# Pool products between the value products, and the eighth square as a second term of the first and last norm's sum

## The chip, the cores and the metric

One core of a Trainium2 chip. The metric is the device time of one execution in microseconds (us); less is better. PE is TensorE's matmul, PEld its weight load, DVE VectorE, ACT ScalarE, SP the queue that issues most DMAs. Times inside the profile count from the start of its span.

## The reference, cut to what matters

Two transformer blocks over one sequence of 256 tokens and 1024 features, in fp32. The change touches the first mixer of the first block and two of its seven RMS norms:

```python
def pool_attn_mixer(h, w_in, pool_w, pool_scale, q_gain, k_gain, w_out):
    u, q, k, v = jnp.split(h @ w_in, [512, 1024, 1536], axis=-1)
    p = multiscale_pool_minus_identity(u)       # 4 groups of 128 channels: mean of the last 2, 4, 8, 16 tokens, minus u
    p = jnp.einsum('bsgc,gcd->bsgd', p.reshape(B, S, 4, 128), pool_w)   # one 128x128 matrix per group
    p = p.reshape(B, S, 512) * pool_scale
    a = moba_attention(q, k, v, q_gain, k_gain) # 8 heads of 64; with 256 tokens plain causal attention
    return jnp.concatenate([p, a], axis=-1) @ w_out

def rms_norm(x, g):
    return x * lax.rsqrt(jnp.mean(x * x, axis=-1, keepdims=True) + EPS) * g
```

Every norm needs, for each token, the sum of the squares of its 1024 features. The first norm stands ahead of this mixer, the last one at the very end of the program.

## The kernel before

**Layout.** Activations lie transposed: features on the 128 partitions, eight blocks of them, tokens along the row (`T` = 256). `X` holds the residual. An fp32 product is made of three fp32r products: a weight tile and an activation are each split into `hi` (an ACT copy) and `lo` (a DVE subtract of `hi` from the source). `mm3` issues hi·hi (L280), hi·lo (L281) and lo·hi (L282) into one accumulator. `split_act` splits an activation: L342 or, with a scale, L336 on ACT, then L322 or L331 on DVE.

**Weights.** They come as a stream of 128x128 tiles in the order in which the program asks for them (`W`, which appends to `order`). Eight tiles are a half chunk p; `w_split(p)` splits it with one ACT cast (L246) and one DVE subtract (L322, 128x1024) into one of `NB` = 5 pairs of buffers hi0/lo0 to hi4/lo4, in rotation. When the first tile of half chunk p is asked for, `W` issues the split of p+4, so that split uses the buffers of half chunk p-1. The splits of half chunks 16 to 20 fall into the stretch of the change and are called split 16 to split 20 here. In the kernel before, half chunk 15 holds the weights of value products k = 6 and 7, and half chunk 16 the four pool weights and the first four of `pa_out`.

**Buffers.** `al` and `alp` take one of 46 SBUF slots, `bk` one of eight PSUM banks, each from the front of a first-in first-out list; `fr` and `bf` put them back at the end. A new holder of a buffer waits until every instruction that uses the former holder is done, those written later in the program included.

**Order.** A scheduler places the instructions when the program is built: for each engine it keeps dependencies and, among those it takes to be ready, prefers the one written first. What stands in an engine's queue then runs in that order. `step` advances the attention by one iteration, and `behind` (with `PINNED`, which is DVE) ties every DVE instruction of that iteration behind the DVE instruction that was written last before it:

```python
        for ins in reversed(done):
            if ins.engine in engines and ins.engine not in last:
                last[ins.engine] = ins.name
```

**The stretch of the change** is in `mixer0`. After the products for k, q and u come the value products: eight steps k, each with two token halves and three products of 512 columns (L285), in banks `vb`. Among them, at k = 0, 2, 4, 6, `windows` makes the pool inputs of one group on DVE (running sums of 2, 4, 8, 16 tokens, times 1/count, minus u). `step` is called after k = 3 (head 0's logits, `att_a(0)`) and after k = 7 (`att_b(0)`: reciprocal and scaling on DVE, transposes on PE, copy on ACT; `att_a(1)`). Then the four pool inputs are split into `px`, `step` is called once more (`att_c(0)`, `att_b(1)`, `att_a(2)`), then for each pair of groups six pool products go into one bank, and four results are split with the pool scale into `pp`. `pp[k]` is the input of `pa_out` for k = 0 to 3, the attention's output that for k = 4 to 7. `acc_begin` takes four banks for `pa_out`: output blocks m = 0,1 in the first, 2,3 in the second, 4,5 in the third, 6,7 in the fourth.

**The norm.** `norm_add(m)` squares block m on ACT (L373) and adds the square to `sacc` on DVE (L322); `norm_sum` multiplies `sacc` with a matrix of 1/1024 (two fp32 matmuls of one column, L285), which sums over the partitions. `self.gain` is None for the first and the last norm alone. In the last one, `turn(m)` scales each block (L1823) and transposes it on PE (L1825) right after `norm_add(m)`.

Of the kernel before, what the change touches and what calls it, by code (L numbers as in the profile page):

```python
# [12 lines left out]
OP = mybir.AluOpType  # L13
# [3 lines left out]
T = 256  # L17
D = 1024
KD = 8
# [117 lines left out]
class Prog:  # L137
# [137 lines left out]

    def mm3(self, out, key, x, start, stop):

        wh, wl = self.W(key)
        mm = self.nc.tensor.matmul
        mm(out, wh, x[0], start=start, stop=False, skip_group_check=True)  # L280
        mm(out, wh, x[1], start=False, stop=False, skip_group_check=True)  # L281
        mm(out, wl, x[0], start=False, stop=stop, skip_group_check=True)  # L282

    def mm(self, out, l, r, start=True, stop=True):
        self.nc.tensor.matmul(out, l, r, start=start, stop=stop, skip_group_check=True)  # L285
# [78 lines left out]
    def norm_add(self, m):  # L364
        nc = self.nc
        acc = self.sacc[:, :T]
        if self.gain is not None:
            self.split_act(self.X[:, m, :], *self.xgo(m), scale=self.gain(m))
        if self.nsq == 0:
            nc.scalar.activation(acc, self.X[:, m, :], AF.Square)  # L370
        else:
            sq = self.sqb[:, (self.nsq % 2) * T:(self.nsq % 2) * T + T]
            nc.scalar.activation(sq, self.X[:, m, :], AF.Square)  # L373
            self.tt(acc, acc, sq, OP.add)
        self.nsq += 1

    def norm_sum(self, sqrt=False):


        b = self.bk()  # L380
        for h in range(2):
            self.mm(b[:, h:h + 1], self.sacc[:, h * 128:h * 128 + 128], self.ones[:, 0:1], h == 0, True)
        self.uid += 1
        v = self.cst([128, 2], f"nv{self.uid}")
        self.ts(v, b[:, 0:2], EPS, OP.add)
        self.bf(b)
        if sqrt:
            y, t = self.cst([128, 2], "nry"), self.cst([128, 2], "nrt")
            self.nc.scalar.activation(y, v, AF.Sqrt)
            self.nc.vector.reciprocal(y, y)  # L390
            self.stt(t, y, -0.5, y, OP.mult, OP.mult)
            self.tt(t, t, v, OP.mult)
            self.stt(y, t, 1.5, y, OP.add, OP.mult)
            self.rtok = y
        else:
            self.rtok = self.rsqrt_small(v, 2, f"nr{self.uid}")
        self.fr(self.sacc, self.sqb)
# [127 lines left out]
    def mixer0(self):  # L525
# [39 lines left out]
        for b in range(4):  # L565
            sq = self.al()
# [34 lines left out]
        for b in range(2):  # L601
            p = self.bk()
            for i in range(2):
                for h in range(2):
                    for g in range(2):
                        o = h * 16 + (2 * b + i) * 2 + g
# [82 lines left out]
                yield  # L689
        self.lanes[0].append(attention())  # L690

        pin = []

        def windows():
            for g in range(4):
                s = self.al(shape=(128, 2, T))
                u = us[g // 2][:, g % 2, :]
                cur = u
                for e in range(g + 1):
                    d = 1 << e  # L700
                    nxt = s[:, e % 2, :]
                    self.tt(nxt[:, d:], cur[:, d:], cur[:, :T - d], OP.add)
                    nc.vector.tensor_copy(nxt[:, :d], cur[:, :d])
                    cur = nxt
                o = s[:, (g + 1) % 2, :]
                self.tt(o, cur, ivs[g // 2][:, (g % 2) * T:(g % 2) * T + T], OP.mult)
                self.tt(o, o, u, OP.subtract)
                pin.append((s, o))
                yield
        win = windows()  # L710
        vb = [self.bk(), self.bk()]
        vt = [self.al() for t in range(2)]
        for k in range(KD):
            wh, wl = self.W(("pa_v", k, 0), n=4)
            for t in range(2):
                xh, xl = (x[:, t * 128:t * 128 + 128] for x in self.hl(hs[k]))
                self.mm(vb[t], xh, wh, k == 0, False)
                self.mm(vb[t], xl, wh, False, False)
                self.mm(vb[t], xh, wl, False, k == KD - 1)
            if k in STEPS0:  # L720
                self.step()
            if k % 2 == 0:
                next(win)
        for t in range(2):
            nc.scalar.activation(vt[t], vb[t], AF.Copy, scale=rtok[:, t:t + 1])
            self.bf(vb[t])
        self.fr(*hs)
        px = []
        for g in range(4):
            x = self.alp()  # L730
            self.split_act(pin[g][1], *self.hl(x))
            self.fr(pin[g][0])
            px.append(x)
        self.fr(*us, *ivs)
        self.step()
        pp = []
        for b in range(2):
            p = self.bk()
            for i in range(2):
                self.mm3(p[:, i * T:i * T + T], ("pool_w", 0, 2 * b + i), self.hl(px[2 * b + i]), i == 0, True)  # L740
            for i in range(2):
                x = self.alp()
                self.split_act(p[:, i * T:i * T + T], *self.hl(x), scale=self.pv("pscale", 2 * b + i))
                pp.append(x)
            self.bf(p)
        self.fr(*px)
        xs = pp + ath
        self.acc_begin()
# [1235 lines left out]
```

## Time and profile before

| | |
|---|---|
| median of 3 runs | 1043.2 us (1041.69 to 1044.56) |
| the profiled execution | 1046.05 us, of which its span 1044.3 us |
| PE busy | 97% of the span |
| DVE, ACT busy | 83%, 58% |
| granted TensorE clock, mean | 0.995 |
| PE's waits between 20 and 100 us | 1.5 us in two pieces |

Busy PE time counts a matmul from its start to its modelled end, and neighbours overlap: products of 256 columns that follow one another closely start every 0.12 us though each is shown as 0.28 us long. So it is the distance of starts that tells whether PE runs dense, and the idle time in brackets that tells where it waited.

### The profile page before, as it was taken

Reading aid. Unit: us, or ns where it says so; the run is one execution under the profiler, and the core shown is the slowest. Engines: PE = TensorE matmul, PEld = TensorE weight load, DVE = VectorE, ACT = ScalarE, POOL = GpSimd, SP = SyncE. Lnnn points to the kernel's source line nnn. Section 1 sums busy time; section 2 is a strip of 40 time slices with the busy share of each in tenths; the row PEclk is TensorE's granted clock in tenths of the full one; section 3 lists DMA queues with packets and bytes.
Section 4 is the critical chain, followed back from the end, with each engine's and each line's share of the span. In section 5 each row is a group of like instructions: output and inputs, shape, how many; then the busy total and the mean of one; then the engine's idle time right before and its main releaser. Section 6 shows DMA issues by size and latency. Waiting matters only on the chain. (4 is left out here: it accounts for less than half of the span.)

```text
span 1044.3 us, 21508 instructions
## 1 busy us (share of the span) xinstructions
PE 1015.2 (97%) x8834; PEld 980.9 (94%) x8834; DVE 865.7 (83%) x1662; ACT 605.3 (58%) x953; POOL 96.8 (9%) x86
## 2 busy tenths in 40 slices
PE   9999999999999999999999999889999999999996
PEld 8879999999999999999999998778999999999996
DVE  6887999997799998999999978997667979775554
ACT  6566665565669975665654687233345457444444
POOL 0000000000000000000295000334200200000000
PEclk9999999999999999999999999999999999999999
DMA  8953367886682263777654644234454464955531
GB/s 310 353 186 119 125 207 272 305 314 223 211 281 95 71 235 120 241 255 269 225 202 153 241 149 149 72 116 146 145 198 162 154 206 142 386 172 192 191 133 41
DMA packets 32499, 202.75 MB, mean 194 GB/s; under 512 B 3601, under 2 KB 5137, under 8 KB 9233
## 3 DMA queue, kind: packets, MB, share of 16 engines
q1 hardware_dynamic: 31392, 199.80, 54.2%
q10 hardware_dynamic: 1008, 1.58, 0.4%
q8 instruction: 69, 1.13, 0.4%
q14 instruction: 30, 0.24, 0.1%
HBM read 200.32 MB, written 1.05 MB: 193 GB/s over the span
## 5 line engine op out<-in xcount | busy, mean ns | idle before, releaser
L281 PE MATMUL b<-s,hi 128*128 128x256 f32 x2192 | 616.9, 282 | 1.8 <-DVE s L331 0.9
L280 PE MATMUL b<-s,hi 128*128 128x256 f32 x2128 | 600.6, 283 | 4.8 <-ACT s L342 3.0
L282 PE MATMUL b<-s,lo 128*128 128x256 f32 x2128 | 598.2, 282 | 4.1 <-DVE lo L322 4.0
L322 DVE TENSOR_TENSOR lo<-raw,hi 128x1024 fp32r<-128x1024 f32 (+1 forms) x309 | 389.8, 1266 | 112.1 <-ACT hi L246 111.2
L246 ACT CAST hi<-raw 128x1024 fp32r<-128x1024 f32 (+1 forms) x309 | 319.8, 1041 | 261.4 <-PE b L281 185.4
L281 PEld LDWEIGHTS b<-s,hi 128*128 128x128 f32 x2192 | 413.4, 189 | 6.0 <-issue 3.0
L280 PEld LDWEIGHTS b<-s,hi 128*128 128x128 f32 x2128 | 400.6, 189 | 12.2 <-issue 4.0
L282 PEld LDWEIGHTS b<-s,lo 128*128 128x128 f32 x2128 | 400.9, 189 | 6.8 <-DVE lo L322 5.8
L322 DVE TENSOR_TENSOR s<-s,s 128x256 f32<-128x256 f32 (+3 forms) x173 | 89.2, 524 | 8.0 <-ACT s L373 3.7
L331 DVE SCALAR_TENSOR_TENSOR s<-b,pvt,s 128x255 f32<-128x255 f32 (+1 forms) x153 | 72.6, 478 | 3.8 <-ACT s L880 2.8
L461 DVE SCALAR_TENSOR_TENSOR ada<-ada,s 128x512 f32<-128x512 f32 x96 | 63.9, 685 | 3.6 <-DMA ada<-in_ada_dram 3.6
L285 PE MATMUL b<-xgh,hi 128*128 128x256 f32 (+1 forms) x212 | 60.5, 285 | 0.0
L285 PE MATMUL b<-s,hi 128*128 128x256 f32 x212 | 59.6, 281 | 0.0
L285 PE MATMUL b<-xgh,lo 128*128 128x256 f32 (+1 forms) x212 | 59.6, 281 | 0.0
L342 ACT CAST s<-s 128x256 fp32r<-128x256 f32 (+1 forms) x77 | 33.0, 440 | 37.0 <-DVE s L322 26.6
L880 ACT ACTIVATE s<-b,pvt 128x256 f32<-128x256 f32 x76 | 42.0, 556 | 8.5 <-PE b L282 8.2
L285 PE MATMUL b<-s,s 128*128 128x256 f32 (+5 forms) x212 | 39.2, 380 | 7.9 <-DVE s L322 7.4
L1174 POOL MEMSET tab<- 128x8 f32 x1 | 0.1, 113 | 494.2 <-DVE ada L461 494.2
L285 PEld LDWEIGHTS b<-s,hi 128*128 128x128 f32 x212 | 40.1, 189 | 0.0
L285 PEld LDWEIGHTS b<-xgh,lo 128*128 128x128 f32 x212 | 40.0, 189 | 0.0
L285 PEld LDWEIGHTS b<-xgh,hi 128*128 128x128 f32 x212 | 39.9, 188 | 0.0
L322 DVE TENSOR_TENSOR s<-s 128x256 f32<-128x256 f32 (+3 forms) x70 | 35.4, 508 | 4.7 <-ACT s L1790 4.3
(367 smaller groups left out, 1042.3 us busy)
## 6 DMA issues: line engine op xcount, KB each, us to landing
raw<-in_wst_dram SPq DMA_DIRECT2D x157, 1024.0 KB, 5.0
ada<-in_ada_dram SPq DMA_DIRECT2D x24, 1024.0 KB, 7.4
raw<-in_wst_dram SPq DMA_DIRECT2D x4, 512.0 KB, 6.4
s<-in_catt_dram SPq DMA_DIRECT2D x8, 192.0 KB, 7.2
s<-in_rgw_dram SPq DMA_DIRECT2D x5, 256.0 KB, 3.7
raw<-in_wst_dram SPq DMA_DIRECT2D x4, 256.0 KB, 5.5
xp<-in_xt_dram ACTq DMA_DIRECT2D x3, 256.0 KB, 6.1
s<-in_cinv_dram SPq DMA_DIRECT2D x2, 256.0 KB, 5.5
```

The source lines that it names most:

```text
L246: self.nc.scalar.copy(h, s)
L280: mm(out, wh, x[0], start=start, stop=False, skip_group_check=True)
L281: mm(out, wh, x[1], start=False, stop=False, skip_group_check=True)
L282: mm(out, wl, x[0], start=False, stop=stop, skip_group_check=True)
L285: self.nc.tensor.matmul(out, l, r, start=start, stop=stop, skip_group_check=True)
L322: self.nc.vector.tensor_tensor(out, a, b, op=op)
L331: self.nc.vector.scalar_tensor_tensor(out, a, s, b, op0=op0, op1=op1)
L342: nc.scalar.copy(hi, src)
L461: self.nc.vector.scalar_tensor_tensor(x, x, 0.5, self.cs[h], op0=OP.mult, op1=OP.mult, accum_out=self.macc[:, h, i:i + 1])
L880: nc.scalar.activation(c[:, i, :], z, AF.Identity, scale=self.pv(f"fcw{l}2", m), bias=self.pv(f"fcb{l}", m))
L1174: g.memset(S[:, :, 0:1], 0.0)
```

## The change

The four pool weights are taken ahead of value products k = 7, and the six pool products of groups 0 and 1 with their splits stand there too; those of groups 2 and 3 follow the value products. The windows move from k = 0, 2, 4, 6 to k = 0, 1, 2, 4, and each window now splits its own input. Half chunk 15 so holds the weights of k = 6 and the pool weights, half chunk 16 those of k = 7. In the first and the last norm the eighth square is not added to `sacc`; `norm_sum` takes it as a second term with two more matmuls.

```diff
@@ -275,7 +275,10 @@
     def mm3(self, out, key, x, start, stop):
-        wh, wl = self.W(key)
+        self.mm3w(out, self.W(key), x, start, stop)
+
+    def mm3w(self, out, w, x, start, stop):
+        wh, wl = w
         mm = self.nc.tensor.matmul
@@ -371,15 +374,18 @@
             nc.scalar.activation(sq, self.X[:, m, :], AF.Square)
-            self.tt(acc, acc, sq, OP.add)
+            if self.nsq < 7 or self.gain is not None:
+                self.tt(acc, acc, sq, OP.add)
...
         b = self.bk()
-        for h in range(2):
-            self.mm(b[:, h:h + 1], self.sacc[:, h * 128:h * 128 + 128], self.ones[:, 0:1], h == 0, True)
+        terms = [self.sacc] if self.gain is not None else [self.sacc, self.sqb[:, T:]]
+        for n, s in enumerate(terms):
+            for h in range(2):
+                self.mm(b[:, h:h + 1], s[:, h * 128:h * 128 + 128], self.ones[:, 0:1], n + h == 0, n == len(terms) - 1)
@@ -705,12 +711,29 @@
                 self.tt(o, o, u, OP.subtract)
-                pin.append((s, o))
+                x = self.alp()
+                self.split_act(o, *self.hl(x))
+                self.fr(s)
+                px.append(x)
                 yield
         win = windows()
         vb = [self.bk(), self.bk()]
         vt = [self.al() for t in range(2)]
+        pp = []
+
+        def pool(b):
+            p = self.bk()
+            for i in range(2):
+                self.mm3w(p[:, i * T:i * T + T], pw[2 * b + i], self.hl(px[2 * b + i]), i == 0, True)
+            for i in range(2):
+                x = self.alp()
+                self.split_act(p[:, i * T:i * T + T], *self.hl(x), scale=self.pv("pscale", 2 * b + i))
+                pp.append(x)
+            self.bf(p)
         for k in range(KD):
+            if k == KD - 1:
+                pw = [self.W(("pool_w", 0, m)) for m in range(4)]
+                pool(0)
             wh, wl = self.W(("pa_v", k, 0), n=4)
@@ -719,30 +742,15 @@
             if k in STEPS0:
                 self.step()
-            if k % 2 == 0:
+            if k in (0, 1, 2, 4):
                 next(win)
+        pool(1)
         for t in range(2):
             nc.scalar.activation(vt[t], vb[t], AF.Copy, scale=rtok[:, t:t + 1])
             self.bf(vb[t])
         self.fr(*hs)
-        px = []
-        for g in range(4):
-            x = self.alp()
-            self.split_act(pin[g][1], *self.hl(x))
-            self.fr(pin[g][0])
-            px.append(x)
         self.fr(*us, *ivs)
         self.step()
-        pp = []
-        for b in range(2):
-            p = self.bk()
...
-            self.bf(p)
         self.fr(*px)
```

## Rows read from the trace of the kernel before

**Rows 1.** Page, busy us (share of the span) and instructions of each engine

```profile
PE 1015.2 (97%) x8834; PEld 980.9 (94%) x8834; DVE 865.7 (83%) x1662; ACT 605.3 (58%) x953; POOL 96.8 (9%) x86
```

**Rows 2.** Waits of PE, 20 to 100 us: total us, times, longest

```profile
PE b L281 <- DVE s L331: 0.9, 1, 0.9
PE b L280 <- ACT s L336: 0.6, 1, 0.6
```

**Rows 3.** Stretches of 5 us: busy us by engine (instructions), clock, DMA

```profile
50.00:55.00 5.00, 5.00 (x25) 3.57 (x22) 5.00 (x15) 2.87 (x7) 0.00 (x0) 1.00 0.90 309
55.00:60.00 5.00, 5.00 (x27) 3.67 (x26) 4.52 (x15) 3.01 (x6) 0.00 (x0) 1.00 0.82 275
60.00:65.00 5.00, 3.50 (x26) 2.90 (x25) 5.00 (x16) 2.60 (x7) 0.00 (x0) 1.00 0.66 264
```

**Rows 4.** Timeline of PE at the pool products: start, us, [idle before]

```profile
58.47 0.40 PE L285 MATMUL b<-lo,s 128*128 128x512 f32 x1
58.80 0.93 PE L285 MATMUL b<-s,s 64*128 64x128 f32 x8
59.66 0.39 PE L280 MATMUL b<-s,hi 128*128 128x256 f32 x1
...
60.36 0.28 PE L282 MATMUL b<-s,lo 128*128 128x256 f32 x1
61.26 0.50 PE L280 MATMUL b<-s,hi 128*128 128x256 f32 x2 [0.62 <-ACT s L336]
62.64 0.39 PE L281 MATMUL b<-s,hi 128*128 128x256 f32 x1 [0.88 <-DVE s L331]
...
63.69 0.27 PE L659 MATMUL b<-cb,s 128*128 128x128 f32 x1
```

**Rows 5.** Timeline of DVE in the same stretch

```profile
56.95 1.22 DVE L322 TENSOR_TENSOR lo<-raw,hi 128x1024 fp32r<-128x1024 f32 x1 [0.48 <-ACT hi L246]
...
59.91 1.21 DVE L322 TENSOR_TENSOR lo<-raw,hi 128x1024 fp32r<-128x1024 f32 x1
...
62.12 0.47 DVE L331 SCALAR_TENSOR_TENSOR s<-b,xp,s 128x256 fp32r<-128x256 f32 x1
62.51 0.41 DVE L322 TENSOR_TENSOR s<-s,s 128x256 f32<-128x256 f32 x1
62.84 0.15 DVE L654 RECIPROCAL s<-s 128x2 f32<-128x2 f32 x1
...
63.62 0.47 DVE L331 SCALAR_TENSOR_TENSOR s<-b,rqky,s 128x256 f32<-128x256 f32 x1
...
64.54 0.41 DVE L322 TENSOR_TENSOR s<-s,s 128x256 fp32r<-128x256 f32 x1
```

**Rows 6.** Timeline of ACT in the same stretch

```profile
58.79 1.03 ACT L246 CAST hi<-raw 128x1024 fp32r<-128x1024 f32 x1
...
64.34 0.48 ACT L661 COPY s<-b 128x384 f32<-128x384 f32 x1 [0.95 <-PE b L659]
```

**Rows 7.** Timeline of PE at the first norm's sum

```profile
27.49 0.50 PE L285 MATMUL b<-cb,s 128*128 128x1 f32 x4
27.85 0.36 PE L280 MATMUL b<-s,hi 128*128 128x256 f32 x1
```

**Rows 8.** Timeline of all engines at the last norm

```profile
1034.64 0.43 DVE L322 TENSOR_TENSOR s<-s,s 128x256 f32<-128x256 f32 x1 [0.55 <-ACT s L373]
...
1035.06 0.44 PE L1825 MATMUL b<-cb,s 128*128 128x128 f32 x2
1035.62 0.42 ACT L373 ACTIVATE s<-xp 128x256 f32<-128x256 f32 x1 [0.61 <-DVE xp L331]
...
1036.48 0.44 PE L1825 MATMUL b<-cb,s 128*128 128x128 f32 x2 [0.99 <-ACT s L1823]
1036.65 0.53 PEld L285 LDWEIGHTS b<-cb,s 128*128 128x128 f32 x4
...
1037.30 0.16 DVE L326 TENSOR_SCALAR nv<-b 128x2 f32<-128x2 f32 x1 [0.81 <-PE b L285]
...
1038.52 1.41 DVE L326 TENSOR_SCALAR s<-b,nry 128x512 f32<-128x512 f32 x2
```

More of the change, by code (lines that the diff above doesn't have):

```diff
@@ L690, in mixer0 @@
         self.lanes[0].append(attention())
-        pin = []
+        px = []
         def windows():
@@ L727, in mixer0 @@
         self.fr(*hs)
-        px = []
-        for g in range(4):
-            x = self.alp()
-            self.split_act(pin[g][1], *self.hl(x))
-            self.fr(pin[g][0])
-            px.append(x)
         self.fr(*us, *ivs)
         self.step()
-        pp = []
-        for b in range(2):
-            p = self.bk()
[L739 to L744, printed above, removed]
-            self.bf(p)
         self.fr(*px)
```

## The prediction

> **What bounds the kernel now.** I read the page's first part, PE's waits, the stretches of 5 us, the timelines. PE is busy for 97% of the span, DVE for 83% [rows 1], so whatever saves time must take away a wait of PE, shorten the dense stream of PE or shorten the chain at the very end. Around this mixer PE waits twice, for pool results, 0.6 and 0.9 us [rows 2]. The timeline shows both: the pool products of groups 0 and 1 run from 59.66 us, the last of them starts at 60.36, and the first `pa_out` products start at 61.26 (when the hi half of `pp[0]` is there) and go on at 62.64 (when its lo half is) [rows 4]. Counted by starts, with one product per 0.12 us, the losses are 61.26 - 60.36 - 0.12 = 0.78 and 62.64 - 61.48 - 0.12 = 1.04: 1.8 us in all. That is the prize of the first part of the change and its limit, for elsewhere in this stage PE runs dense. The stretches name the second actor: DVE is busy without a gap from 50 to 55 us and from 60 to 65 us, and for 4.52 of 5 us between, while PE falls to 3.50 of 5 us [rows 3]. So the pool results are late because DVE is behind, not because their products stand late in PE's queue. The clock stays at its upper level throughout.
>
> **First norm.** The removed add (0.4 us of DVE) shortens nothing, as PE waits for nothing from 20 us to 60 us [rows 2]. But two more fp32 matmuls stand in a dense PE stream. Two cost four PE instructions; from the first of them to the next ordinary product it is 27.85 - 27.49 = 0.36 us, with 0.50 shown as busy [rows 7]. Cost: +0.4 us (0.36 to 0.5), all on the path.
>
> **Last norm.** Now the last square ends at 1035.62 + 0.42 = 1036.04; then ACT scales the last block, PE transposes it at 1036.48, loads for the sum begin at 1036.65, and the sum is read at 1037.30, 0.65 us after that load [rows 8]. The add of the eighth square runs beside the scaling, so it is not by itself what the end waits for. With the square as a term of its own, the old term's sum is complete at 1034.64 + 0.43 = 1035.07 and can be multiplied after the transposes at 1035.06 to 1035.50, when PE has nothing else; the new term can start at about 1036.07 and be read at 1036.07 + 0.65 = 1036.72. Gain: 1037.30 - 1036.72 = 0.6 us. The last transposes slip by under 0.1 us and have until 1038.52 - 0.6 = 1037.9 [rows 8]. Bounds: -0.6, or, if the sums stay behind the transposes in PE's queue, 0 to +0.4 (four more instructions). I take -0.6, since the square is ready 0.4 us before the transposes are. The page "PSUM — Partial Sum Buffer" of the Trainium skill (Engine vs sequencer instructions) states that matmuls start and complete in program order; by it the queue's order fixed at build time decides, and a sum queued behind the transposes would give the upper bound.
>
> **Pool products, step by step.** (a) *DVE.* By 62.84 DVE has done all four windows, the lo halves of `px[0]` to `px[2]`, that of `pp[0]` and splits 16 to 20. After the change the split of `px[3]` no longer stands behind the value products. To finish it DVE needs the same list without split 20 (1.14 to the next start, 1.21 busy) and `pp[0]` (62.51 - 62.12 = 0.39), with `px[3]` added (0.33 to 0.41), and perhaps without the one gap of 0.48 [rows 5]: 62.84 - 1.14 - 0.39 + 0.33 = 61.6, or 61.2 with the gap filled. I take 61.4. `pp[0]`'s lo half ends near 61.8, 0.7 us earlier than now, `pp[1]`'s at 62.2; if both go first, `px[3]` is done at 62.2. So moving the products ahead does not by itself remove the wait: DVE still has that list.
>
> (b) *Split 20, the new wait.* It uses the buffers of half chunk 15. Those were free after the last value product; now they hold the pool weights, so they are free only after the last pool product of groups 2 and 3, which needs `px[3]`: 61.4 + 6 x 0.12 = about 62.2. From the last value product to the end of split 20 it now takes from 58.8 (58.47 + 0.40, less overlap) to 61.1 (59.91 + 1.21) [rows 4, 5], the ACT cast at 58.79 between [rows 6]: 2.3 us. So split 20 ends at about 64.5. Queued behind it is the attention: `W` for value product 7 writes split 20 just ahead of the `step` after k = 7, and `behind` ties `att_b(0)` and `att_a(1)` on DVE to the last DVE instruction written. Their first instruction, the reciprocal, starts at 62.84 now [rows 5]; it would start at 64.5, 1.7 us later. DVE meanwhile idles for about a microsecond while ACT casts.
>
> (c) *Who waits for that.* Counting the bank list through the program, `pa_out`'s four banks are, after the change, those of `att_b(0)` (m = 0,1), `att_a(1)` (m = 2,3), the second pool pair (m = 4,5) and the first value half (m = 6,7). Only the last is free at once; before, two were. Relative to the reciprocal the others are freed at 63.62 + 0.47 - 62.84 = 1.25 (`att_a(1)`'s logits read) and 64.34 + 0.48 - 62.84 = 1.98 (`att_b(0)` copied) [rows 5, 6], hence at 65.75 and 66.5; the pool pair after the reductions that end 64.54 - 62.84 = 1.70 behind it and two splits of 0.39, near 67. The Trainium skill ("Perfetto Trace Analysis", Matmuls) wants independent groups of matmuls to rotate through different banks so that evacuations overlap; by it this order is a loss, and the sum would be the one below.
>
> (d) *Sum for PE.* Work that needs nothing new ends at 60.48 now; `att_a(2)` (half of the 0.86 us from 58.80 to 59.66) must wait for the first pool pair's bank, so at 60.05. The first new work starts at 61.4: 1.35 us lost. Then there are six pool products, six of `pa_out` k = 0 and six of k = 1 for m = 6,7 (0.72 each) and `att_a(2)` (0.43): 2.6 us, up to 64.0. Next are `att_b(0)`'s transposes, which follow the reciprocal by 63.69 - 62.84 = 0.85 [rows 4, 5], at 65.35: another 1.35 us lost. From 65.75 on the banks come free faster than PE fills them. Lost: 2.7 us against 1.8 now, **+0.9 us**. Bounds: -1.8 (no wait left), and +1.7 if both `pp` splits go ahead of `px[3]` (0.8 later).
>
> DMAs: the weight stream keeps its length, and the exchange of four tiles moves no issue. Attention biases go to slots that are free long before; that costs nothing.
>
> **Sum.** +0.4 - 0.6 + 0.9 = +0.7 us. Against the profiled execution, 1046.05 (span 1044.3 and 1.75 around it): 1046.75. The profiled run lies 2.85 above the median of the three timed runs, so for the median 1043.2 + 0.7 = 1043.9.
>
> **Rivals.** *The prize is had in full.* The splits of `pp` fit into gaps of DVE's dependent chains, pool products and splits are ready before 60.5, and split 20 delays nothing that PE needs. For it: `px[0]` and `px[1]` are split much earlier than now. Against it: DVE is full [rows 3]. -1.8 + 0.4 - 0.6 = -2.0: 1041.2.
>
> *The attention's lateness is carried to the end of the mixer (slower).* Place: the last step of attention feeds `pa_out` k = 7. Each of its iterations is tied behind splits of later half chunks, which are themselves freed by `pa_out` products. If the 1.7 us of (b), up to 2.5 in the worse case of (a), is not caught up while PE has other `pa_out` products, PE waits once more there. Price: 1.7 on top of +1.7 + 0.4 - 0.6 = +3.2: 1046.4. It decides from the point where the products of k = 4 to 6 run out before k = 7's input is there. Against it: PE shows no wait between 62.64 and 100 us [rows 2], so there is some stock of products.
>
> *The last norm's sum keeps its place behind the transposes:* +0.9 + 0.4 + 0.4 = +1.7: 1044.9.
>
> **How the numbers follow.** Forecast (old wait exchanged for the new one) 0.56, full prize 0.25, attention late to the end 0.11, last norm unchanged 0.08. About 0.3% (3.1 us) is what a measurement of this kernel tells from no change; the runs shown scatter by 1.4 us about their median. The forecast and the last rival lie inside; of the full prize a seventh (0.04) may be measured beyond it; of the late attention a half, with 0.02 from the forecast's upper end, gives 0.08. Faster 0.04, same 0.88, slower 0.08. The range runs from the full prize, 1041.2, to the late attention, 1046.4; both bounds of the pool stage lie in it.
>
> **What would show it.** Right: split 20's subtract after the last pool product and some 3 us later than 59.91; the reciprocal right behind it; a wait of PE for DVE or ACT after the first `pa_out` products of one bank; eight instructions where the first norm's sum had four; the last sum read under 0.7 us after the last square. Wrong: no wait of PE over 0.3 us between 58 and 68 us, or the reciprocal ahead of split 20. A wait of PE near 90 us would speak for the slower rival.

## The result and the profile after

| | before | after |
|---|---|---|
| median (range) of runs | 1044.66 us (1041.58 to 1048.48, 10 runs) | 1050.29 us (1047.88 to 1055.4, 10 runs) |
| ratio, 95% interval | | 1.0066 (1.0051 to 1.0081) |
| the profiled execution, its span | 1046.05 us, 1044.3 us | 1049.39 us, 1047.4 us |
| mean granted clock of it | 0.995 | 0.993 |

The kernel became slower: by 0.66%, thus 6.9 us, by the ratio of the runs, and by 5.6 us by the medians. Forecast were +0.7 us and a range that ended at 1046.4. Line numbers after are shifted: L280, L281, L282 and L285 of before are L283, L284, L285 and L288; L322 is L325, L326 is L329, L331 is L334, L336 is L339, L342 is L345, L373 is L376, L654 is L660, L659 is L665, L1825 is L1833; L246 stays.

Waits of PE from 20 to 130 us after (total, times, longest), beside which [rows 2] had 0.9 and 0.6:

```profile
PE b L283 <- ACT s L339: 1.3, 1, 1.3
PE b L665 <- DVE s L329: 1.1, 1, 1.1
PE b L288 <- DVE nr132y L334: 0.2, 1, 0.2
```

Timeline of PE after, where [rows 4] is that of before (start, us, operation, idle before and its releaser):

```profile
59.76 0.92 PE L288 MATMUL b<-s,s 64*128 64x128 f32 x4
60.61 0.38 PE L283 MATMUL b<-s,hi 128*128 128x256 f32 x1
...
62.37 0.92 PE L288 MATMUL b<-s,s 64*128 64x128 f32 x4
63.22 0.38 PE L284 MATMUL b<-s,hi 128*128 128x256 f32 x1
...
64.03 0.41 PE L285 MATMUL b<-s,lo 128*128 128x256 f32 x2
65.74 0.39 PE L283 MATMUL b<-s,hi 128*128 128x256 f32 x1 [1.31 <-ACT s L339]
67.24 0.87 PE L665 MATMUL b<-cb,s 128*128 128x128 f32 x3 [1.11 <-DVE s L329]
...
68.18 0.41 PE L284 MATMUL b<-s,hi 128*128 128x256 f32 x1
68.40 0.41 PE L285 MATMUL b<-s,lo 128*128 128x256 f32 x1
```

Timeline of DVE in the same stretch, for [rows 5]:

```profile
63.11 0.42 DVE L325 TENSOR_TENSOR s<-s,s 128x256 fp32r<-128x256 f32 x1 [0.47 <-ACT s L345]
65.35 1.22 DVE L325 TENSOR_TENSOR lo<-raw,hi 128x1024 fp32r<-128x1024 f32 x1 [1.81 <-ACT hi L246]
66.49 0.16 DVE L660 RECIPROCAL s<-s 128x2 f32<-128x2 f32 x1
```

And of ACT, for [rows 6]:

```profile
62.68 0.40 ACT L345 CAST s<-s 128x256 fp32r<-128x256 f32 x1 [0.88 <-DVE s L325]
64.27 1.04 ACT L246 CAST hi<-raw 128x1024 fp32r<-128x1024 f32 x1 [1.19 <-PE b L284]
```

Stretches of 5 us (length, busy time of PE, PEld, DVE, ACT and POOL with instructions, granted clock, DMA share, GB/s), after; before, the clock was 1.00 in [rows 3] and from there to 75 us:

```profile
60.00:65.00 5.00, 4.30 (x26) 3.10 (x25) 2.91 (x10) 2.93 (x8) 0.00 (x0) 1.00 0.63 248
65.00:70.00 5.00, 3.15 (x11) 2.26 (x12) 3.40 (x10) 2.41 (x8) 0.00 (x0) 0.68 0.04 16
...
165.00:170.00 5.00, 4.63 (x26) 4.63 (x27) 5.00 (x17) 1.76 (x2) 0.00 (x0) 0.66 0.32 87
```

Timeline of PE at the first norm after, for [rows 7] (eight instructions where four stood):

```profile
27.32 0.95 PE L288 MATMUL b<-cb,s 128*128 128x1 f32 x8
28.13 0.36 PE L283 MATMUL b<-s,hi 128*128 128x256 f32 x1
```

PE at the second norm's sum, before and then after:

```profile
109.39 0.50 PE L285 MATMUL b<-cb,s 128*128 128x1 f32 x4
113.93 0.50 PE L288 MATMUL b<-cb,s 128*128 128x1 f32 x4
```

And of all engines at the last norm, for [rows 8]:

```profile
1039.09 0.50 PE L288 MATMUL b<-cb,s 128*128 128x1 f32 x4
1039.36 0.42 ACT L376 ACTIVATE s<-xp 128x256 f32<-128x256 f32 x1 [0.60 <-DVE xp L334]
...
1039.82 0.61 PE L288 MATMUL b<-cb,s 128*128 128x1 f32 x4 [0.23 <-ACT s L376]
1040.29 0.41 PE L1833 MATMUL b<-cb,s 128*128 128x128 f32 x2
1040.47 0.16 DVE L329 TENSOR_SCALAR nv<-b 128x2 f32<-128x2 f32 x1 [1.21 <-PE b L288]
```

What the reader is to see. The new wait is there as forecast: split 20's subtract at 65.35, the reciprocal right behind it, PE idle before it. Counted by starts PE loses 65.74 - 64.15 - 0.12 = 1.47 and 67.24 - 65.74 - 0.12 = 1.38, so 2.85 us (2.7 forecast) against 1.81 before. Two things were not forecast. The logits of heads 1 and 2 stood side by side before and took 59.66 - 58.80 = 0.86 us for eight instructions [rows 4]; now each four stand alone and take 0.85. And in the second piece of the wait, at 66.8 us, the granted clock falls to its lower level, 1.2 GHz (0.5), and stays there for 3.4 us: products of 256 columns start every 0.21 us (68.18, 68.40) and not every 0.12. A second fall comes at 165.8 us behind a wait of 1.99 us for weights; before, a wait of 1.3 at that place had no fall behind it.

The stage can be timed from PE's first instruction of the first norm's sum to that of the second's: 109.39 - 27.49 = 81.90 us before and 113.93 - 27.32 = 86.61 after, 4.71 more. All times "of the stage" below are taken like that.

The two profiled executions can't be subtracted from one another beyond that: that of before had falls at 675 and 706 us, that of after at 66.8, 165.8 and 705. In one fall a dense stream gets through 3.4 / 0.21 = 16 products, which take 16 x 0.12 = 1.9 us at the upper level: 1.5 us lost. The timed executions tell how common falls are: their mean granted clock is 0.9920 after (10 runs) and 0.9935 to 0.9938 before (four groups of 11 to 30 runs). One fall lowers the mean by 3.4 x 0.5 / 1045 = 0.0016, so after has about one fall more per execution. The scatter of these means leaves that uncertain by nearly one fall.

### The profile page after: what moved, and what is told of

Its sections match the earlier page's. It is cut to its first block, busy times and chain, and to the rows that moved or that the text cites. A ratio compares the mean times of both kernels' runs of the same rounds, so it can differ in the third digit from the quotient of the medians.

```text
span 1047.4 us, 21521 instructions
## 1 busy us (share of the span) xinstructions
PE 1019.6 (97%) x8842; PEld 985.4 (94%) x8842; DVE 865.1 (83%) x1660; ACT 605.9 (58%) x953; POOL 94.7 (9%) x86
## 5 line engine op out<-in xcount | busy, mean ns | idle before, releaser
L284 PE MATMUL b<-s,hi 128*128 128x256 f32 x2192 | 617.9, 283 | 0.8 <-DVE s L325 0.6
L283 PE MATMUL b<-s,hi 128*128 128x256 f32 x2128 | 602.0, 284 | 5.0 <-ACT s L345 2.0
L285 PE MATMUL b<-s,lo 128*128 128x256 f32 x2128 | 599.0, 283 | 3.3 <-DVE lo L325 3.0
L325 DVE TENSOR_TENSOR lo<-raw,hi 128x1024 fp32r<-128x1024 f32 (+1 forms) x309 | 389.1, 1264 | 115.5 <-ACT hi L246 114.9
L246 ACT CAST hi<-raw 128x1024 fp32r<-128x1024 f32 (+1 forms) x309 | 320.0, 1041 | 267.7 <-PE b L284 192.1
L284 PEld LDWEIGHTS b<-s,hi 128*128 128x128 f32 x2192 | 414.0, 189 | 4.8 <-issue 3.0
L283 PEld LDWEIGHTS b<-s,hi 128*128 128x128 f32 x2128 | 401.5, 189 | 13.5 <-issue 4.5
L285 PEld LDWEIGHTS b<-s,lo 128*128 128x128 f32 x2128 | 401.7, 189 | 5.0 <-DVE lo L325 4.5
L325 DVE TENSOR_TENSOR s<-s,s 128x256 f32<-128x256 f32 (+3 forms) x171 | 87.2, 518 | 9.2 <-ACT s L345 4.9
L334 DVE SCALAR_TENSOR_TENSOR s<-b,pvt,s 128x255 f32<-128x255 f32 (+1 forms) x153 | 72.2, 475 | 4.6 <-ACT s L888 3.9
L288 PE MATMUL b<-xgh,hi 128*128 128x256 f32 (+1 forms) x212 | 60.5, 285 | 0.0
L288 PE MATMUL b<-xgh,lo 128*128 128x256 f32 (+1 forms) x212 | 59.6, 281 | 0.0
L288 PE MATMUL b<-s,hi 128*128 128x256 f32 x212 | 59.6, 281 | 0.0
L345 ACT CAST s<-s 128x256 fp32r<-128x256 f32 (+1 forms) x77 | 32.9, 439 | 36.7 <-DVE s L325 26.9
L288 PE MATMUL b<-s,s 128*128 128x256 f32 (+4 forms) x212 | 39.2, 353 | 7.8 <-DVE s L325 7.2
L325 DVE TENSOR_TENSOR s<-s 128x256 f32<-128x256 f32 (+4 forms) x70 | 36.5, 524 | 4.6 <-ACT s L1798 4.2
L288 PEld LDWEIGHTS b<-s,hi 128*128 128x128 f32 x212 | 40.1, 189 | 0.0
L288 PEld LDWEIGHTS b<-xgh,lo 128*128 128x128 f32 x212 | 40.0, 189 | 0.0
L288 PEld LDWEIGHTS b<-xgh,hi 128*128 128x128 f32 x212 | 39.9, 188 | 0.0
```

The costliest lines, as they stand in the source:

```text
L246: self.nc.scalar.copy(h, s)
L325: self.nc.vector.tensor_tensor(out, a, b, op=op)
L334: self.nc.vector.scalar_tensor_tensor(out, a, s, b, op0=op0, op1=op1)
L345: nc.scalar.copy(hi, src)
```

## The experiments

All ratios are to the kernel before, run beside it on the same chip.

**One half of the change alone.** First the two norms, on the kernel before:

```diff
-            self.tt(acc, acc, sq, OP.add)
+            if self.nsq < 7 or self.gain is not None:
+                self.tt(acc, acc, sq, OP.add)
...
+        terms = [self.sacc] if self.gain is not None else [self.sacc, self.sqb[:, T:]]
...
```

> The kernel before with the norm part alone. Theory (the loss comes from the pool part: split 20 stands late, the attention is tied behind it, PE waits and its clock then falls): the norm part is worth +0.4 at the first norm and -0.6 at the last, so a ratio of 0.999 to 1.001 and no fall of the clock near 67 us. Rival (two more matmuls in the dense stream shift everything that follows against the DMAs and cause the later waits): a ratio of 1.003 or more.

Measured 1046.07 us, 1.001 (0.9995 to 1.0025). Its attention stage is that of before, with the same waits of 0.9 and 0.6 us, yet in this execution the clock fell at 64.7 us. So a fall can follow the wait of before too, in some executions. The stage takes 112.23 - 28.35 = 83.88 us here, 1.98 more than before; 0.45 of it are the first norm's four instructions (below), so with the same work and the same waits this fall cost 1.53 us. Stretch of 5 us of this kernel:

```profile
65.00:70.00 5.00, 5.00 (x29) 4.26 (x28) 3.44 (x13) 2.38 (x9) 0.00 (x0) 0.69 0.00 0
```

Then the pool part alone (the changed kernel with `norm_add` and `norm_sum` of before):

```diff
-            if self.nsq < 7 or self.gain is not None:
-                self.tt(acc, acc, sq, OP.add)
+            self.tt(acc, acc, sq, OP.add)
...
-        terms = [self.sacc] if self.gain is not None else [self.sacc, self.sqb[:, T:]]
...
```

> The change without its norm part. Theory: nearly the whole loss, a ratio of 1.005 to 1.008 against the kernel before, waits of PE of about 2.4 us between 64 and 68 us and the clock at its lower level for some 3.4 us from about 67 us. Rival (norm part): ratio under 1.003.

Measured 1048.84 us, 1.0041 (1.0026 to 1.0056). Waits 1.3 and 1.1 us, clock fall at 66.9, as after. The pool part is the larger loss, 4.3 of 6.9 us by the ratios.

**What in the pool part costs.** Undo the place of split 20 alone, by taking value product 7's weights ahead of the pool weights:

```diff
         for k in range(KD):
+            wh, wl = self.W(("pa_v", k, 0), n=4)
             if k == KD - 1:
                 pw = [self.W(("pool_w", 0, m)) for m in range(4)]
                 pool(0)
-            wh, wl = self.W(("pa_v", k, 0), n=4)
```

> The change with one thing undone: the weights of value product 7 are taken ahead of the pool weights, as in the kernel before, so that split 20 needs only the value products to be done; banks and the tie of the attention stay. Theory: split 20's subtract ends by 63 us, the reciprocal starts by 63.5 us in place of 66.5, PE waits under 1 us between 60 and 70 us, no fall of the clock there, and a ratio of 0.998 to 1.001. Rival (the banks of the accumulators alone make the wait): PE still waits over 2 us, ratio 1.004 or more.

Measured 1046.45 us, 1.002 (1.0004 to 1.0036). Timeline of DVE:

```profile
61.83 1.22 DVE L325 TENSOR_TENSOR lo<-raw,hi 128x1024 fp32r<-128x1024 f32 x1
64.02 0.16 DVE L660 RECIPROCAL s<-s 128x2 f32<-128x2 f32 x1
```

And of PE:

```profile
62.80 0.38 PE L283 MATMUL b<-s,hi 128*128 128x256 f32 x1 [0.15 <-ACT s L339]
63.83 0.92 PE L288 MATMUL b<-s,s 64*128 64x128 f32 x4 [0.65 <-DVE s L334]
64.68 0.39 PE L284 MATMUL b<-s,hi 128*128 128x256 f32 x1
```

With split 20 early the wait is 0.8 us and the clock doesn't fall near 67. So the weights' order carries the wait, the fall and 4.8 of the 6.9 us by the ratios. Note that the two logits still stand apart.

Is it the tie of the attention behind split 20? Leave split 20 late, but write the step ahead of it:

```diff
                 pw = [self.W(("pool_w", 0, m)) for m in range(4)]
+                self.step()
                 pool(0)
...
-            if k in STEPS0:
+            if k in STEPS0 and k < KD - 1:
                 self.step()
```

> The change with the attention step of k = 7 written ahead of the pool weights, so that its DVE instructions are tied behind the windows only, while split 20 stays late. Theory (the tie carries the loss): the reciprocal starts by 63 us although split 20 still ends near 66 us; PE waits under 1.2 us between 60 and 70 us, no fall of the clock there, ratio 0.998 to 1.002. Rival (the late split itself starves PE of weights): PE waits for the lo half of weights near 66 us, and the ratio stays at 1.004 or more.

Measured 1050.44 us, 1.0063 (1.0045 to 1.0081). The expected gain isn't there. The reciprocal is early (61.73), but PE still waits 1.8 us near 63 us, in four smaller pieces, and another 1.0 near 98 us; and the clock falls again, at 64.9, for 6.8 us. The first of these waits ends with the DVE instruction that reads the logits (61.81 to 62.28), and the step's DVE work now stands ahead of the split of `px[3]`, which comes later than after (63.84 against 63.11). So this edit exchanges one delay for another, and what the tie alone is worth stays open. PE timeline:

```profile
62.33 0.38 PE L283 MATMUL b<-s,hi 128*128 128x256 f32 x1 [1.07 <-DVE s L334]
...
63.46 0.44 PE L665 MATMUL b<-cb,s 128*128 128x128 f32 x2 [0.27 <-DVE s L329]
64.31 0.39 PE L284 MATMUL b<-s,hi 128*128 128x256 f32 x1 [0.29 <-DVE s L325]
64.74 2.99 PE L288 MATMUL b<-s,s 128*64 128x256 f32 x8
```

The last row is eight fp32 products that take 1.71 us at the upper level (as at 73.31 after).

Is it the banks? Give `pa_out` the banks of the value halves first:

```diff
         self.fr(*px)
         xs = pp + ath
+        self.banks.rotate(-3)
+        f = [self.banks.popleft() for _ in range(2)]
+        self.banks.rotate(3)
+        self.banks.extendleft(reversed(f))
         self.acc_begin()
```

> The changed kernel with one edit: the first and second bank that `pa_out`'s accumulators take are the two value halves' banks, which are free before any of the attention's. Theory (the late split holds the attention and with it the banks; PE has products left but no bank for them): with two free banks PE has twelve more products (some 1.4 us) that wait for nothing, so the waits between 63 and 70 us fall from 2.6 us to 1.2 or less, no fall of the clock near 67 us follows, and the time falls by 1.5 to 3 us, to a ratio of 1.003 to 1.005 against the kernel before. Rival (inputs are late, not banks: PE waits for the lo half of `px[3]` and the pool results, whatever banks are free): waits stay above 2 us, the ratio stays at 1.0055 to 1.008.

Measured 1050.58 us, 1.0058 (1.0037 to 1.0079): the rival's ratio. Timeline of PE:

```profile
68.15 0.50 PE L283 MATMUL b<-s,hi 128*128 128x256 f32 x2 [1.40 <-ACT s L339]
69.64 0.87 PE L665 MATMUL b<-cb,s 128*128 128x128 f32 x3 [0.99 <-DVE s L329]
```

And of DVE:

```profile
68.90 0.16 DVE L660 RECIPROCAL s<-s 128x2 f32<-128x2 f32 x1
```

The first logits stand at 60.70 here and at 59.76 after, so this execution is 0.94 later from the start. The reciprocal is 2.41 later, so 1.5 us later by the stage's own time: the products that have a bank now stand ahead of the last pool products in PE's queue, split 20 waits for those, and the wait only moves. So free banks alone don't help: what ends the wait is still the chain from the last pool product over split 20.

**Wait or clock.** Fill the wait with work that nobody needs and leave all dependencies:

```diff
         pool(1)
+        fb = self.bk()
+        for i in range(20):
+            self.mm(fb[:, :T], px[0][:, 0, :128], self.hl(px[3])[1], i == 0, i == 19)
+        self.bf(fb)
+        self.banks.appendleft(self.banks.pop())
```

> The changed kernel with twenty products of 256 columns added behind the pool products, into a bank that nobody reads (20 x 0.12 = 2.4 us of work that isn't needed). Dependencies and order stay. Theory (a part of the loss is the clock that falls after the wait: products start every 0.21 us instead of 0.12 for 3.4 us, about 1.6 us): PE waits under 1 us between 63 and 70 us, the clock stays at 1.00 there, and though work was added the time falls by 1 to 2 us against the changed kernel, to a ratio of 1.004 to 1.006. Rival (the clock costs nothing that matters, the attention's late chain alone sets the time): the time is that of the changed kernel within 0.5 us, or longer by as much as the added products delay the rest, up to 2.4 us: ratio 1.0065 to 1.009.

Measured 1047.3 us, 1.0032 (1.0019 to 1.0045). PE timeline:

```profile
64.46 2.52 PE L288 MATMUL b<-s,s 128*128 128x256 f32 x20
...
67.55 0.61 PE L665 MATMUL b<-cb,s 128*128 128x128 f32 x3 [0.34 <-DVE s L329]
```

The stretch of 5 us behind it:

```profile
65.00:70.00 5.00, 4.66 (x33) 3.77 (x33) 3.36 (x10) 2.73 (x8) 0.00 (x0) 1.00 0.12 39
```

The transposes that end the wait start no earlier than after (67.55 against 67.24 us, in an execution that runs 0.32 later), and yet the kernel is faster by 0.34% than the changed one, with 2.4 us of work added. In this stretch the clock is 1.00 where it was 0.68, and the stage takes 113.14 - 27.63 = 85.51 us where it took 86.61. This shows that a part of the loss is the clock behind the wait and not the wait itself. The gain by the ratios is 3.4 us (their intervals are 1.4 and 1.6 us wide to each side), more than one fall's 1.5. The timed executions have a mean granted clock of 0.9943 against 0.9920, by the sum above some 1.4 falls fewer, thus about 2.2 us; and this profile lacks the wait for weights at 165 us and the fall behind it.

**The pair of logits.** With the weights' order put right, write the third step ahead of `pool(1)`, with a free bank for its logits:

```diff
-        pool(1)
         for t in range(2):
             nc.scalar.activation(vt[t], vb[t], AF.Copy, scale=rtok[:, t:t + 1])
...
+        bn = self.banks
+        bn[1], bn[3] = bn[3], bn[1]
         self.step()
+        pool(1)
```

> The kernel with value product 7's weights taken first, and in addition the third attention step written ahead of the second pool pair, with a bank that is free, so that the logits of heads 1 and 2 stand side by side on PE again, as in the kernel before. Theory (two heads' logits side by side take 0.86 us for eight instructions, as before; apart they take 0.85 for each four): the eight stand near 60.5 us and take 0.86, attention products between 30 and 112 us fall by 0.84, the time falls by about 0.8 us against the same kernel without this edit (ratio 1.002), to 1.001 to 1.0015. Rival (the shorter row is only a matter of how the profile models ends, or the gain turns into a wait for pool results): ratio 1.002 or more, waits of PE between 58 and 70 us up by 0.8.

```profile
59.92 0.93 PE L288 MATMUL b<-s,s 64*128 64x128 f32 x8
60.78 0.38 PE L283 MATMUL b<-s,hi 128*128 128x256 f32 x1
...
62.83 0.39 PE L283 MATMUL b<-s,hi 128*128 128x256 f32 x1 [0.19 <-ACT s L748]
```

PE timeline: eight in 0.86 us again, and the only wait left is 0.19 us. The stage takes 109.49 - 27.44 = 82.05 us, and without the pair (weights' order alone) 111.18 - 28.01 = 83.17: the pair is worth 0.84 by its own rows and about 1.1 here. The timed ratio, 1.0025 (1.0011 to 1.0039), doesn't show it.

In the changed kernel itself the same edit:

> The changed kernel with the third attention step written ahead of the second pool pair and with a free bank, so that the logits of heads 1 and 2 stand side by side again; split 20 stays late. Theory (lost pair 0.84 us, wait some 1 us more than before, clock fall 1.7 us after it): the pair stands near 60 us with 0.86 us for eight instructions; the wait grows by up to 0.84 as PE has that much less work ahead of it, so the time stays within 1 us of the changed kernel: ratio 1.0055 to 1.0075. Rival (the lost pair alone makes the loss): ratio under 1.004.

```profile
60.23 0.93 PE L288 MATMUL b<-s,s 64*128 64x128 f32 x8
66.00 0.50 PE L283 MATMUL b<-s,hi 128*128 128x256 f32 x2 [0.84 <-ACT s L339]
67.50 0.63 PE L665 MATMUL b<-cb,s 128*128 128x128 f32 x3 [1.00 <-DVE s L329]
```

Measured 1051.4 us, 1.0076 (1.0056 to 1.0095), level with the changed kernel. The eight take 0.87 us again (the next product starts at 61.10), yet the stage takes 114.66 - 27.81 = 86.85 us, no less than after (86.61). The transposes start as late, 39.69 us behind the first norm's sum against 39.92, since they follow split 20; and PE waits 1.6 us more in three pieces at 95 to 99 us, for the attention, which after doesn't. So the lost pair alone isn't the loss: where split 20 is late, putting it right brings nothing.

**The norms' terms.** The last norm's second term alone (the edit is made on the kernel with both norm terms; `norm_add` likewise), and then pair, order and that term together:

```diff
-        terms = [self.sacc] if self.gain is not None else [self.sacc, self.sqb[:, T:]]
+        terms = [self.sacc] if self.gain is not None or not self.late else [self.sacc, self.sqb[:, T:]]
+        self.late = True
...
```

> The kernel before with the last norm's second term alone (first norm as before, pool products as before). Theory: the end is 0.57 us shorter, as in the changed kernel's trace, and all else the same: ratio 0.9995 (0.998 to 1.001). Rival (the term costs something elsewhere): ratio over 1.001.

> The kernel with value product 7's weights first and the logits side by side, with the second term in the last norm alone (the first norm as before). Theory: first norm -0.45 against the same kernel with both terms, so a ratio of 1.0005 to 1.001, within the measurement of the kernel before; PE's waits in the stage no longer than before's, so no gain from the moved pool products either. Rival (the moved pool products bring the wait's 1.8 us once split, banks and pairs are put right): ratio under 0.9985.

Measured 1043.01 us, 0.9991 (0.9979 to 1.0003), and 1045.62 us, 0.9996 (0.9983 to 1.001). The first agrees with the 0.57 us of the rows. The second says that the moved pool products are worth nothing that can be measured once their side effects are undone, and cost nothing. Its profile tells where their prize went: PE's waits in the stage fell from 1.50 to 0.48 us, but the stage only from 81.90 to 108.95 - 27.32 = 81.63, since the same products, from start to start, take 0.75 us longer in the new order.

The edits of order, banks and the last norm's term together, on the changed kernel, with the logits apart:

> The changed kernel with value product 7's weights taken ahead of the pool weights, `pa_out`'s first two banks those of the value halves, and the second term in the last norm alone. If the late split and the banks are the whole cost of the first part: waits of PE under 0.8 us between 58 and 70 us against 1.8 by starts in the kernel before, clock at 1.00 there, ratio 0.998 to 0.9995. If something else in the moved order costs (as the 2 us that were left with the weights' order alone), the ratio stays at 1.001 to 1.0025.

Measured 1046.24 us, 1.0021 (1.0007 to 1.0035). Here the bank order did bring a wait of its own, 2.0 us in three pieces at 89 to 96 us, for copies of `att_b`.

The term of the first norm in the changed kernel, taken away (by the same edit as for the last norm's term alone), and then its four PE instructions put back without its data (the old sum issued twice, into columns that nobody reads):

```diff
...
+        if twice:
+            for h in range(2):
+                self.mm(b[:, 2 + h:3 + h], self.sacc[:, h * 128:h * 128 + 128], self.ones[:, 0:1], False, True)
```

> The changed kernel with the first norm as before (its eighth square added on DVE, two fp32 matmuls); the rest of the change stays. Theory (the first norm's second term costs what its rows show, 0.45 us, and no more): ratio 1.006, within the interval of the changed kernel (1.0051 to 1.0081). Rival (the term costs more than its rows: with and without it, three pairs of kernels differ by 0.19, 0.25 and 0.29%): ratio 1.003 to 1.0045.

> The same as the one without the first norm's second term, but its two fp32 matmuls are issued a second time into columns that nobody reads: the four PE instructions are back, without the other input. If the four instructions are the cost, the time is that of the changed kernel (ratio 1.0066); if it hangs on the second input or on the add that left DVE, it is that of the kernel without the term.

Measured 1048.42 us, 1.0046 (1.0028 to 1.0064), and 1050.9 us, 1.0063 (1.0042 to 1.0083). The two differ by 0.17%, which points to the four instructions and not the data, but their intervals overlap, so it isn't shown. Four pairs of kernels that differ in this term put it at 0.19, 0.29, 0.20 and 0.17%: about 2 us, where the row shows 0.81 - 0.36 = 0.45. Each pair has an interval of some 0.2% to either side, and the last two share a kernel. In all four the mean granted clock of the timed executions is lower with the term: 0.9932 against 0.9943, 0.9932 against 0.9938, 0.9920 against 0.9935 and 0.9923 against 0.9935, thus 0.4 to 0.9 falls or 0.6 to 1.4 us. Each of these differences is about as large as the scatter of the means, but all four point the same way. So a good part of what the row lacks may be more falls of the clock.

Where the rest arises isn't the same in the profiles. In the pair with the logits put right, 0.54 us at the second norm's sum became 2.26 at the third's (300.75 against 298.49), across a wait of 1.9 us for weights near 160 us that the other execution didn't have. That wait is there with the term and not without it in three of the four pairs. In the last two kernels neither has it; the difference was 0.14 at the second norm's sum and 0.40 at the third's, and then three clock falls came behind 570 us, one of 6.8 us, against one. The wait isn't the term's alone: before has it too (1.3 us) without the term.

**Filling the wait of before.** Twelve unneeded products behind the pool products of the kernel before, with the last norm's term:

```diff
...
+        for i in range(12):
+            self.mm(fb[:, :T], px[1][:, 0, :128], self.hl(px[1])[0], i == 0, i == 12 - 1)
...
```

> The kernel before with the second term in the last norm alone (ratio 0.9991) and twelve products of 256 columns, whose result nobody reads, behind the pool products, where PE waits 1.8 us for pool results: 1.4 us of work put into the wait. Theory (the clock falls in some executions of the kernel before too, as at 64.7 us in the profile of the first norm's run and at 63 us in that of the last norm's, after this wait, and costs 1.6 us each time): no fall near 63 us, time shorter by 0.5 to 1.5 us, ratio 0.9975 to 0.9985. Rival (a fall is rare in the timed executions of the kernel before): ratio 0.999 to 1.000.

Measured 1046.77 us, 1.002 (1.0002 to 1.0037). The theory got the stage right (no wait from 58 to 75 us, clock 1.00 there, 82.33 us for the stage) and the time wrong: by the two ratios the kernel is 0.3% slower than without the products (0.9991), give or take 0.2%. Filling paid where the wait was 2.85 us; where it was 1.8 it didn't. Like with the first norm's term, some half a microsecond in the stage ended as 2 to 3, and the cause is open.

## Why the prediction was wrong

**Right in mechanism, and in size partly by luck: steps (b) and (d), the wait.** Split 20 waits for the last pool product, the reciprocal is right behind it, PE idles 2.85 us by starts (2.7 forecast, 1.81 before). The delays inside were larger: the split of `px[3]` was done at 63.5 (61.4 forecast), the reciprocal came at 66.49 (64.5). Step (a) took DVE as full. It was idle instead, 2.91 of 5 us busy from 60 to 65: after the moved windows each thing waits for the next (window, ACT's cast, subtract, product, ACT's cast of split 20), so the round trips set the time and not DVE's list. The sum of the waits survived since PE too was later than forecast, among other things by 0.84 us for logits; that the two delays nearly cancel is luck. By the clock of the span the transposes came at 67.24 and not at 65.35.

**Wrong in its reason: step (c), the banks.** With two banks given that are free at once the waits stayed 1.4 and 1.0 us. What held was when split 20's buffers come free: with the weights' order undone the waits were 0.15 and 0.65 us. The share of the tie between split 20 and the attention wasn't isolated.

**Failed, mis-sized: the logits.** Step (d) counted `att_a(2)` as half of the 0.86 us that eight instructions take. Alone, four take 0.85. So each half costs twice what was put down, +0.84 us in all that the sum lacked.

**Failed, a term put at nothing: the clock.** The sum priced the wait at its length. Behind its first piece the clock fell, and that is a term of its own, 1.53 us where the same stage ran with and without a fall; the timed executions have about one fall more than before, and the kernel with the wait filled is 0.34% faster. The sentence that the clock stays at its upper level throughout was true of this stage in the one profile read of before, which had falls at 675 and 706 us; two other executions with the same stage had one in it, at 63 and 65 us.

**First norm: +0.4, at its place right (0.45), by the end wrong.** Four pairs put it at about 2 us. A part of the other 1.5 us may be more falls of the clock; what brings them and where the rest comes from is not shown.

**Last norm: -0.6, right.** The sum is read 1040.47 - 1039.78 = 0.69 us after the last square (under 0.7 forecast; 1.26 before): -0.57.

**The rivals.** The full prize was far off. The late attention was there (its last result 98.10 against 92.24 us), but PE had other products and shows no wait near 90 us, so in the changed kernel that rival is refuted as a mechanism, though its sign was right. Its mechanism does exist: in four of the runs above (the step moved, the banks, the banks with order and last term, the pair in the changed kernel) PE waited 0.5 to 2.5 us at 89 to 101 us, for the attention's results.

Put together: of the 4.71 us by which the stage grew, the wait is 1.04, the logits 0.84, the first norm's term 0.45 and the fall up to 1.5; some 0.9 is spread over products that start a little later each in the new order. With the last norm's -0.57 that makes +4.1, against 5.6 by the medians and 6.9 by the ratio (5.3 to 8.5). The remaining 1.2 to 4.4 us lie behind the stage. In the profile of after the stretch from the second to the third norm's sum is 2.75 us longer than before, with the longer wait for weights at 165 us and a fall behind it; later stretches are shorter, among them one with one fall fewer. One profile of each can't tell how common that is, so this part is measured but not explained.

## What to carry to other kernels

In a kernel whose PE is dense, don't price a wait of PE at its length alone: look for the granted clock in the stretches behind it, in more than one profiled execution. The clock isn't all either: with the weights' order undone the mean clock was 0.9946 against 0.9935 before, and the kernel was still 0.2% slower. When a step moves in a stream of weights, ask which buffer now holds what, since a split that waits for late work holds all that is queued behind it on DVE. And before halving a row that stands for two groups of instructions, look for a row where one group stands alone.

## What the runs showed of the hardware

Products that contract over 64 partitions run beside those of the other 64: even heads lie on partitions 0 to 63 and odd ones on 64 to 127, and the logits of heads 1 and 2 took 0.86 us together (before, and nearly the same again at 59.92 and 60.23 us above) and 0.85 each when apart. The Trainium skill ("TensorEngine Tiling (Array Packing)", Key Properties) states that tiles of the array work independently and can load weights and multiply in parallel; the rows agree, with a factor of 1.98.

A granted clock of 0.5, thus 1.2 GHz, came with two waits of 1.3 and 1.1 us with one product between them. It lasted 3.4 us there (6.8 in other profiles), and products took about 1.75 times as long: eight fp32 ones 2.99 us for 1.71 at the upper level, and 0.21 us for 0.12 between starts of the others. The same waits came with it in some executions only: the stage of before had no fall in the profile shown and one in two others, of kernels that differ in the norms alone, behind 0.6 and 0.9 us. The Trainium skill ("TensorE: Matmul & The Clock Gate", Part 1) gives this clock gate these two levels and none between; all rows read here have 1.00 or 0.50, or a mean of the two over a stretch.
